# Sliding-window copy on one core: partitions by batch, channel half and 16-row band, and stores as 8 KB row scatters

## The chip, the core and the metric

The kernel runs on one core of a Trainium2 chip. The metric is device time in microseconds (µs), from the start of the program to its end. One execution was also taken by the hardware profiler; its span is the stretch that the profile covers.

## What is computed

The input is x of 16 batches, 64 channels, 64 rows and 64 columns in float32 (16.78 MB). A window of 8 by 8 moves over it with a stride of 4 in both directions, which gives 15 by 15 windows. The output holds each window for all channels (58.98 MB). No number is changed; the work is a gather.

```python
batch, c, h, w = (16, 64, 64, 64); window_size = 8; stride = 4
n_h = n_w = 15
for i in range(n_h):
    for j in range(n_w):
        result[:, i, j] = x[:, :, 4*i:4*i+8, 4*j:4*j+8]   # -> [16, 15, 15, 64, 8, 8]
```

In the output, one batch and one window (i, j) are 64 channels of 64 numbers that lie together: 16 KB. Neighbouring windows overlap, so each input number is written about 3.5 times.

## The kernel before

The 128 partitions stand for 16 batches times 8 groups of 8 channels. Tile `L` holds the whole input: each partition has 8 channels of 64 rows. Two loads on the SP queue fill it (L41 and L42): first the upper 32 rows of every channel, then the lower 32.

Two nested loops run over i and j. For each window VectorE copies the 8 channels by 8 rows by 8 columns of every partition from `L` into a packed tile `g` (L50). Then the tile is stored with one DMA of 256 KB (L51). In it each partition writes 2 KB that lie together in the output. The stores alternate between the SP and the ACT queue. 28 buffers of `g` go round, so the copy of window k waits until the store of window k-28 has landed. ScalarE computes nothing, GpSimd only sets a few constants at the start, and TensorE has no work.

A queue issues in order: a store on SP stands behind the two loads and behind every earlier store on SP.

Of the kernel before, what the change touches and what calls it, by code (L numbers as in the profile page):

```python
# [1 line left out]

# [4 lines left out]


@with_exitstack  # L10
def kernel(
    ctx: ExitStack,
    tc: tile.TileContext,
    x: bass.AP,
    window_size: int,
    stride: int,
    out: bass.AP,
):
    nc = tc.nc
    P = nc.NUM_PARTITIONS  # L20

    B, C, H, W = x.shape
    Bo, NH, NW, Co, WSo, WSo2 = out.shape
    WS = int(window_size)
    ST = int(stride)
    assert Bo == B and Co == C and WSo == WS and WSo2 == WS

    f32 = mybir.dt.float32

    CHI = P // B  # L30
    CLO = C // CHI
    assert CHI * B == P and CLO * CHI == C

    lpool = ctx.enter_context(tc.tile_pool(name="lpool", bufs=1))
    gpool = ctx.enter_context(tc.tile_pool(name="gpool", bufs=28))

    L = lpool.tile([P, CLO, H, W], f32)

    HHALF = H // 2
    x_v = x.rearrange("b (ch cl) h w -> b ch cl h w", ch=CHI)  # L40
    nc.sync.dma_start(out=L[:, :, 0:HHALF, :], in_=x_v[:, :, :, 0:HHALF, :])  # L41
    nc.sync.dma_start(out=L[:, :, HHALF:H, :], in_=x_v[:, :, :, HHALF:H, :])  # L42

    trig = [nc.sync, nc.scalar]
    k = 0
    for i in range(NH):
        for j in range(NW):
            g = gpool.tile([P, CLO, WS, WS], f32, name="g")
            src = L[:, :, i * ST : i * ST + WS, j * ST : j * ST + WS]
            nc.vector.tensor_copy(out=g[:, :, :, :], in_=src)  # L50
            trig[k % 2].dma_start(out=out[:, i, j, :, :, :], in_=g[:, :, :, :])  # L51
            k += 1


# [1 line left out]
_INS = ['x', 'window_size', 'stride']  # L56
_OUTS = [((16, 15, 15, 64, 8, 8), 'float32')]
#: Inputs that are plain numbers.
_NUMBERS = {'window_size': 8, 'stride': 4}


# [26 lines left out]
```

## Time and profile before

| | |
|---|---|
| Median of 9 runs | 220.88 µs (220.25 to 222.49) |
| The profiled execution: own time, span | 219.09 µs, 217.3 µs |
| Moved | 75.83 MB: 16.78 MB read, 58.98 MB written |
| Mean over the span | 349 GB/s |
| VectorE busy | 89.1 µs (41% of the span), 225 copies |
| ScalarE, TensorE busy | no instructions that count as busy |

In the views of the profile, "DMA share" is the mean busy share of the core's 16 DMA engines in a stretch, and may stand a little over 1 where packets overlap. "GB/s" is what they moved in it. A packet is one piece that lies together in memory at both ends: 8 KB in the loads and 2 KB in the stores here. A name with "q" (SPq, ACTq) is the queue on which an engine issues DMAs. The profiled execution lies 1.79 µs above its span, and 0.8% under the median of the runs.

### The profile page before, as it was taken

What the parts mean: (1) busy time and instruction counts of PE and PEld (TensorE: products, weight loads), DVE (VectorE), ACT (ScalarE), POOL (GpSimd) and SP (SyncE); (2) the same over time, 40 slices, a digit from 0 to 9 for tenths busy, and PEclk for the clock granted to TensorE, in tenths of its full rate; (3) what the DMA queues carried; (4) which work ended last, traced back from release to release, by engine and by line L of the source; (5) the groups of instructions that cost most, each with busy time, mean ns of one, the idle gap of its engine ahead of it and who ended that gap; (6) DMA issues with size and microseconds to landing.
All of it is one profiled execution on the core that took longest, in us unless ns stands there. A gap on an engine that the chain in (4) does not pass through costs nothing.

```text
span 217.3 us, 824 instructions
## 1 busy us (share of the span) xinstructions
DVE 89.1 (41%) x225; POOL 0.2 (0%) x4
## 2 busy tenths in 40 slices
DVE  0000791124532444554655545555564556550000
POOL 0000000000000000000000000000000000000000
DMA  6999999989995999999999999999999999999996
GB/s 210 425 427 419 425 417 426 421 314 322 330 332 172 294 304 351 359 363 358 357 369 354 361 347 358 351 350 350 347 358 342 352 356 359 351 362 352 330 348 235
DMA packets 34487, 75.83 MB, mean 349 GB/s; under 512 B 3632, under 2 KB 3632, under 8 KB 32432
## 3 DMA queue, kind: packets, MB, share of 16 engines
q1 hardware_dynamic: 18352, 46.41, 58.9%
q10 hardware_dynamic: 16128, 29.37, 39.6%
q14 instruction: 7, 0.06, 0.1%
HBM read 16.78 MB, written 58.98 MB: 349 GB/s over the span
## 4 chain that ended last, share of the span: by engine, by line
DMA 82%; DVE 7%; issue 1%; DVEq 0%; ACTq 0%
DMA out_dram<-g 72%; DMA L<-in_x_dram 10%; DVE g L50 7%; DVEq L50 0%; ACTq L51 0%
## 5 line engine op out<-in xcount | busy, mean ns | idle before, releaser
L50 DVE COPY g<-L 128x512 f32<-128x512 f32 x225 | 89.1, 425 | 107.0 <-DMA out_dram<-g 82.1
L69 POOL MEMSET const-bfloat16-1.0<- 128x1 bf16 x1 | 0.1, 102 | 0.0
L69 POOL MEMSET const-uint8-127<- 128x1 uint8 x1 | 0.1, 102 | 0.0
L69 POOL MEMSET const-float32-1.0<- 128x1 f32 x1 | 0.1, 99 | 0.0
L69 POOL MEMSET const-float32-0.0<- 128x1 f32 x1 | 0.1, 98 | 0.2 <-issue 0.2
## 6 DMA issues: line engine op xcount, KB each, us to landing
out_dram<-g SPq DMA_DIRECT2D x113, 256.0 KB, 5.5
out_dram<-g ACTq DMA_DIRECT2D x112, 256.0 KB, 5.1
L<-in_x_dram SPq DMA_DIRECT2D x2, 8192.0 KB, 33.8
```

The source lines that it names most:

```text
L50: nc.vector.tensor_copy(out=g[:, :, :, :], in_=src)
L69: nc = _bacc.Bacc("TRN2", target_bir_lowering=False, num_devices=1)
```

## The change

**Layout.** Partition p now stands for batch p/8, channel half (p/4) mod 2 and a band q = p mod 4 of 16 rows. Each partition of `L` holds 32 channels by 16 rows by 64 columns. 16 loads of 1 MB fill it: for each chunk of 8 channels (in the order 2, 0, 1, 3) one for each band, the even bands on SP and the odd ones on ACT. Such a load goes to every fourth partition, 32 of them, in pieces of 4 KB.

**Windows.** An instruction now makes four windows of one column j at once, one for each band: i = 4q + s with the slot s from 0 to 3. So there are 15 x 4 = 60 steps in place of 225. The slots 0 to 2 lie inside the band and are copied by ScalarE (L112). Slot 3 takes its upper 4 rows from the partition's own band (VectorE, L114) and its lower 4 from the next partition's first rows, through VectorE's `stream_shuffle` (L115). In slot 3 the band 3 has no window (i would be 15).

**Stores.** A step's tile is 8 KB in each partition, which lie together in the output. GpSimd stores it with an indirect DMA (L125): 128 rows of 8 KB, each to the row that `idx` names. `idx` is worked out once at the start by 11 small VectorE instructions on a 128x1 tile (L63 to L78). In slot 3 the rows of band 3 get a number beyond the bounds, and are not stored.

**Start and end.** The first 8 steps are made in two halves of 16 channels (stores of 0.5 MB with rows of 4 KB): the first halves need only the chunks 0 and 1. The second halves follow two by two between whole steps. The last two steps are stored from SP in 4 and 3 pieces of 32 partitions (L119). Their tiles reuse the buffers of the third and second last step before them. Nine buffers of 1 MB (`G_101` to `G_109`) go round.

The diff, without the arithmetic of `idx`:

```diff
-    nc.sync.dma_start(out=L[:, :, 0:HHALF, :], in_=x_v[:, :, :, 0:HHALF, :])
-    nc.sync.dma_start(out=L[:, :, HHALF:H, :], in_=x_v[:, :, :, HHALF:H, :])
-    trig = [nc.sync, nc.scalar]
-    for i in range(NH):
-        for j in range(NW):
-            g = gpool.tile([P, CLO, WS, WS], f32, name="g")
-            nc.vector.tensor_copy(out=g[:, :, :, :], in_=src)
-            trig[k % 2].dma_start(out=out[:, i, j, :, :, :], in_=g[:, :, :, :])
...
+    x_v = x.rearrange("b (ch cl) (hq r) w -> hq (b ch) cl (r w)", ch=CH, hq=HQ)
+    for k in (2, 0, 1, 3):
+        for q in range(HQ):
+            (nc.sync, nc.scalar)[q % 2].dma_start(
+                out=L[q::HQ, k * cw : (k + 1) * cw, :, :],
+                in_=x_v[q, :, k * cw : (k + 1) * cw, :],
+            )
...
+    order = [(j, s) for j in range(NW) for s in range(NSLOT)]
+    TAIL, BACK = 2, 3
...
+    def window(j, s, half):
...
+        if not last:
+            nc.scalar.copy(out=g, in_=L[:, cs, s * ST : s * ST + WS, cols])
+        else:
+            nc.vector.tensor_copy(out=g[:, :, 0:ST, :], in_=L[:, cs, s * ST : RB, cols])
+            nc.vector.stream_shuffle(out=g[:, :, ST:WS, :], in_=L[:, cs, 0:ST, cols], mask=nxt)
+        if (j, s) in order[-TAIL:]:
+            g_q = g.rearrange("(m q) c r w -> q m (c r w)", q=HQ)
+            for q in range(HQ - 1 if last else HQ):
+                free(nc.sync.dma_start(out=o_q[q * NSLOT + s, j], in_=g_q[q]))
+            return
...
+        st = nc.gpsimd.indirect_dma_start(
+            out=o,
+            out_offset=bass.IndirectOffsetOnAxis(ap=ix[:, 0:1], axis=0),
+            in_=g.rearrange("p c r w -> p (c r w)"),
...
+    EARLY = 8
+    for j, s in order[:EARLY]:
+        window(j, s, 0)
...
+    at -= 2 * BACK
+    for w in rest[-TAIL:]:
+        window(*w, None)
```

On the ACT queue the start reads as follows, before (-) and after (+). `L` is the input tile, `G_101` and so on are the nine store buffers, and the shapes are those of what is moved:

```order
-L51 DMA out_dram<-g 16x8x512 x112
...
+L52 DMA L<-in_x_dram 32x8x1024 x8
+L112 ACT_TABLE_LOAD
+L112 COPY G_101<-L 128x1024 x2
+L112 COPY G_102<-L 128x1024
+L112 COPY G_103<-L 128x1024 x2
+L112 COPY G_104<-L 128x1024
```

The 112 stores are gone from ACT. It now issues half of the loads, and then makes the copies of the slots 0 to 2.

On the GpSimd queue, which stored nothing before, the stores stand in this order behind the start (`idx_hlast` and `idx_h` are the row numbers of the half stores, with band 3 left out and with it; `idx` is that of the whole ones):

```order
8 L125 DMA out_dram<-G_102,idx_hlast 14400x1024 [waits DVE_49]
9 L125 DMA out_dram<-G_104,idx_hlast 14400x1024 [waits DVE_49]
10 L125 DMA out_dram<-G_101,idx_h 14400x1024 [waits Activation_49] x2
11 L125 DMA out_dram<-G_102,idx_h 14400x1024 [waits Activation_49]
12 L125 DMA out_dram<-G_103,idx_h 14400x1024 [waits Activation_49] x2
13 L125 DMA out_dram<-G_104,idx_h 14400x1024 [waits Activation_49]
14 L125 DMA out_dram<-G_105,idx_h 14400x1024 [waits DMASW0_49,Activation_49]
```

The two stores that VectorE makes come first, then six of ScalarE's; from the ninth store on, each also waits until the store eight places before it has landed.

On SP the stores of every other window are replaced by half of the loads and by the seven pieces at the end:

```order
-L41 DMA L<-in_x_dram 128x8x2048
-L42 DMA L<-in_x_dram 128x8x2048
-L51 DMA out_dram<-g 16x8x512 x113
...
+L52 DMA L<-in_x_dram 32x8x1024 x8
+L119 DMA out_dram<-G_102 16x2x2048 x4
+L119 DMA out_dram<-G_103 16x2x2048 x3
```

SP goes from 115 DMAs to 15, and its stores come last.

More of the change, by code (lines that the diff above doesn't have):

```diff
@@ L28 @@
     f32 = mybir.dt.float32
-    CHI = P // B
-    CLO = C // CHI
-    assert CHI * B == P and CLO * CHI == C
-    lpool = ctx.enter_context(tc.tile_pool(name="lpool", bufs=1))
[L35 to L41, printed above, removed]
-    nc.sync.dma_start(out=L[:, :, HHALF:H, :], in_=x_v[:, :, :, HHALF:H, :])
@@ L44 @@
-    trig = [nc.sync, nc.scalar]
-    k = 0
-    for i in range(NH):
-        for j in range(NW):
-            g = gpool.tile([P, CLO, WS, WS], f32, name="g")
[L49 to L52, printed above, removed]
+    i32 = mybir.dt.int32
+    ALU = mybir.AluOpType
+    HQ = 4
+    CH = P // (B * HQ)
+    CL = C // CH
@@ new lines @@
+    RB = H // HQ
+    NSLOT = RB // ST
+    NWIN = NH * NW
+    CFREE = CL * WS * WS
+    assert HQ == 4 and CH == 2 and WS == 2 * ST
+    lpool = ctx.enter_context(tc.tile_pool(name="lpool", bufs=1))
+    ipool = ctx.enter_context(tc.tile_pool(name="ipool", bufs=1))
+    gpool = ctx.enter_context(tc.tile_pool(name="gpool", bufs=1))
+    L = lpool.tile([P, CL, RB, W], f32)
+    x_v = x.rearrange("b (ch cl) (hq r) w -> hq (b ch) cl (r w)", ch=CH, hq=HQ)
+    NCH = 4
+    cw = CL // NCH
+    for k in (2, 0, 1, 3):
[4 more added lines that the diff above has]
+            )
@@ new lines, in itile @@
+    def itile(name):
+        return ipool.tile([P, 1], i32, name=name)
+    pi, tb, tq, tc_, idx, idx_last = (itile(n) for n in ("pi", "tb", "tq", "tc", "idx", "idx_last"))
+    nc.gpsimd.iota(pi[:, :], pattern=[[0, 1]], base=0, channel_multiplier=1)
+    nc.vector.tensor_scalar(out=tb[:, :], in0=pi[:, :], scalar1=3, scalar2=None, op0=ALU.logical_shift_right)
+    nc.vector.tensor_scalar(out=tc_[:, :], in0=pi[:, :], scalar1=2, scalar2=1, op0=ALU.logical_shift_right, op1=ALU.bitwise_and)
+    nc.vector.tensor_scalar(out=tq[:, :], in0=pi[:, :], scalar1=HQ - 1, scalar2=None, op0=ALU.bitwise_and)
@@ new lines @@
+    nc.vector.tensor_scalar(out=tb[:, :], in0=tb[:, :], scalar1=float(NWIN * CH), scalar2=None, op0=ALU.mult)
+    nc.vector.tensor_tensor(out=tb[:, :], in0=tb[:, :], in1=tc_[:, :], op=ALU.add)
+    nc.vector.tensor_scalar(out=tc_[:, :], in0=tq[:, :], scalar1=float(NSLOT * NW * CH), scalar2=None, op0=ALU.mult)
+    nc.vector.tensor_tensor(out=idx[:, :], in0=tb[:, :], in1=tc_[:, :], op=ALU.add)
+    nc.vector.tensor_scalar(out=tq[:, :], in0=tq[:, :], scalar1=float(HQ - 1), scalar2=float(2 * B * NWIN * CH), op0=ALU.is_equal, op1=ALU.mult)
@@ new lines @@
+    nc.vector.tensor_tensor(out=idx_last[:, :], in0=idx[:, :], in1=tq[:, :], op=ALU.add)
+    HCL = CL // 2
+    idx_h, idx_hlast = itile("idx_h"), itile("idx_hlast")
+    for d, e in ((idx_h, idx), (idx_hlast, idx_last)):
+        nc.vector.tensor_scalar(out=d[:, :], in0=e[:, :], scalar1=2.0, scalar2=None, op0=ALU.mult)
+    o_v = out.rearrange("b i j (ch cl) r w -> (b i j ch) (cl r w)", ch=CH)
+    o_h = out.rearrange("b i j (ch cl) r w -> (b i j ch) (cl r w)", ch=2 * CH)
+    nxt = [min(p + 1, 31) for p in range(32)]
@@ new lines, with free @@
+    order = [(j, s) for j in range(NW) for s in range(NSLOT)]
+    TAIL, BACK = 2, 3
+    o_q = out.rearrange("b i j (ch cl) r w -> i j b ch (cl r w)", ch=CH)
+    def free(st):
+        tc.declare_no_dep(st.ins, group="stores", reason="each store writes rows of its own")
+        tc.add_to_no_dep_group("stores", st.ins)
+    UNITS = 18
+    G = [gpool.tile([P, 2 * HCL, WS, WS], f32, name=f"G{n}") for n in range(UNITS // 2)]
+    at = 0
+    def window(j, s, half):
+        nonlocal at
+        cols = slice(j * ST, j * ST + WS)
+        last = s == NSLOT - 1
+        if half is None:
+            n, c0 = 2, 0
+            at += at % 2
+        else:
+            n, c0 = 1, half * HCL
+        u = at % UNITS
+        at += n
+        cs = slice(c0, c0 + n * HCL)
+        g = G[u // 2][:, u % 2 * HCL : (u % 2 + n) * HCL, :, :]
+        if not last:
+            nc.scalar.copy(out=g, in_=L[:, cs, s * ST : s * ST + WS, cols])
+        else:
+            nc.vector.tensor_copy(out=g[:, :, 0:ST, :], in_=L[:, cs, s * ST : RB, cols])
[5 more added lines that the diff above has]
+            return
+        if half is None:
+            o, ix = o_v, (idx_last if last else idx)
+        else:
+            o, ix = o_h, (idx_hlast if last else idx_h)
+        st = nc.gpsimd.indirect_dma_start(
+            out=o,
+            out_offset=bass.IndirectOffsetOnAxis(ap=ix[:, 0:1], axis=0),
+            in_=g.rearrange("p c r w -> p (c r w)"),
+            in_offset=None,
+            element_offset=(s * NW + j) * CH * CFREE + (half or 0) * HCL * WS * WS,
+            bounds_check=B * NWIN * CH * (1 if half is None else 2) - 1,
+            oob_is_err=False,
+        )
+        free(st)
@@ L56 @@
+    EARLY = 8
+    for j, s in order[:EARLY]:
+        window(j, s, 0)
+    late = list(order[:EARLY])
+    rest = list(order[EARLY:])
+    while late:
+        for w in late[:2]:
+            window(*w, 1)
+        for w in rest[:2]:
+            window(*w, None)
+        late, rest = late[2:], rest[2:]
+    for w in rest[:-TAIL]:
+        window(*w, None)
+    at -= 2 * BACK
+    for w in rest[-TAIL:]:
+        window(*w, None)
 _INS = ['x', 'window_size', 'stride']
```

## The prediction

> **What bounds the kernel now.** I read the page first, then the chain of waits, then the busy time by stretches, and last the issues of the stores.
>
> ```profile
> DVE 89.1 (41%) x225; POOL 0.2 (0%) x4
> DMA packets 34487, 75.83 MB, mean 349 GB/s; under 512 B 3632, under 2 KB 3632, under 8 KB 32432
> HBM read 16.78 MB, written 58.98 MB: 349 GB/s over the span
> DMA out_dram<-g 72%; DMA L<-in_x_dram 10%; DVE g L50 7%; DVEq L50 0%; ACTq L51 0%
> L50 DVE COPY g<-L 128x512 f32<-128x512 f32 x225 | 89.1, 425 | 107.0 <-DMA out_dram<-g 82.1
> ```
>
> VectorE works 41% of the span and waits 82.1 µs for stores to free its buffers; 82% of the chain that ended last is DMA. So the rate of the transfers bounds it, and the question is what that rate is in each stage. The stretches say it (columns: from:to, length, VectorE busy and count, GpSimd busy and count, a clock that does not matter here, DMA share, GB/s):
>
> ```profile
> 2.00:3.00 1.00, 0.00 (x0) 0.00 (x0) 1.00 0.95 156
> 3.00:4.00 1.00, 0.00 (x0) 0.00 (x0) 1.00 0.87 360
> 10.00:23.00 13.00, 0.00 (x0) 0.00 (x0) 1.00 1.01 423
> 23.00:45.00 22.00, 11.10 (x32) 0.00 (x0) 1.00 1.02 423
> 45.00:50.00 5.00, 1.71 (x4) 0.00 (x0) 1.00 0.82 285
> 50.00:100.00 50.00, 22.48 (x58) 0.00 (x0) 1.00 0.96 315
> 100.00:200.00 100.00, 53.81 (x131) 0.00 (x0) 1.00 1.03 355
> 200.00:215.00 15.00, 0.00 (x0) 0.00 (x0) 1.00 1.00 340
> 215.00:216.00 1.00, 0.00 (x0) 0.00 (x0) 1.00 0.46 174
> 216.00:217.30 1.30, 0.00 (x0) 0.00 (x0) 1.00 0.00 0
> ```
>
> Four things are to be seen. Loading runs at 423 GB/s. Storing alone runs at 355, with the engines just as full: a store packet simply takes longer for its bytes. In 45 to 100 the engines are not full. And little moves in the first 4 µs and the last 2.
>
> Packet times follow as share x 16 engines x bytes / rate. A load packet takes 1.01 x 16 x 8192 / 423 = 313 ns; a store packet takes 1.03 x 16 x 2048 / 355 = 95 ns, where a quarter of 313 would be 78. A line through both gives 22 ns for a packet and 35.5 ns for each KB (28 GB/s for one engine).
>
> The start: 156 + 360 KB by 4.0 µs are 1.2 µs at 423, so 2.8 µs are lost. The end: 174 KB after 215 are 0.5 µs at 355, so 1.8 µs are lost. The hole: 285 for 5 µs and 315 for 50, against 355, lose 1.0 + 5.6 = 6.6 µs. Its cause is an order on a queue:
>
> ```profile
> SPq L51 <- DMA out_dram<-g: 77.8, 28, 56.2
> L51 SPq DMA_DIRECT2D out_dram<-g x113: 538/1213/1757, 58.4 to 212.6; - x113
> L51 ACTq DMA_DIRECT2D out_dram<-g x112: 546/728/1427, 24.1 to 195.4; - x112
> 0.73 0.68 SPq L41 DMA_DIRECT2D L<-in_x_dram  x1
> ```
>
> SP issues its first store only at 58.4 µs, so ACT stores alone until then. An issue (min/median/max in ns) takes 0.54 to 1.76 µs. From the first load's issue at 0.73 to its first bytes (156 of 423 GB/s in the slice 2:3, so from 2.6) pass 1.9 µs.
>
> **The change part by part.**
>
> *Loads, 16.78 MB.* Each is now 4 KB packets to 32 partitions, where it was 8 KB to all 128. By the line a 4 KB packet takes 22 + 142 = 164 ns, which is 400 GB/s. Bounds: 355, the rate of the stores, which also split 16 ways by batch with partitions stepped, and 423. I take 390, between the line and the low end: 43.0 µs (39.7 to 47.3). Sixteen issues of 0.68 µs on two queues are 5.4 µs a queue and run ahead of the bytes.
>
> [...]
>
> *Stores, 58.98 MB.* 225 stores of 2 KB packets become 50 whole and 16 half scatters, and 7 pieces from SP. Almost all bytes go as 8 KB packets from 128 partitions. By the line such a packet takes 313 ns, or 423 GB/s; if the slowness of stores lies in writing and not in the packet, it stays at 355. Nothing before shows an 8 KB store. I take 415: the loads are its nearest row in packet size and partitions, less 2% for the half scatters with 4 KB rows. That is 142 µs (139.4 to 166.1).
>
> *The seam.* The first halves need the chunks 2, 0 and 1, three quarters of the loads: 2.8 + 12.58/0.390 = 35.1 µs. VectorE's copy and shuffle of 128x512 take 0.43 µs each by L50's 425 ns (the shuffle is not in the trace: 0.43 to 0.9), the issue 1.2, the way to the first bytes 1.9: stores begin near 39 µs. By then 14.1 MB are loaded, and 2.7 MB of chunk 3 with 3.9 MB of half stores keep the engines going for 16 µs, to 55. Chunk 3 has landed by about 50 even if it shares the engines equally; a copy, an issue and the way add 0.85 + 1.2 + 1.9 = 4 µs. So one stream hands over to the other with about a microsecond to spare: 0 to 4 µs of hole, I take 1.5, in place of the 6.6 now. `ACT_TABLE_LOAD` and the eleven index instructions stand there while the loads run, and cost nothing while VectorE's two stores go first.
>
> *ScalarE's copies.* A 128x2048 copy has four times the elements of L50's: 1.7 µs at that speed; ScalarE has no row, so up to twice that, 3.4. Three stand in four steps, 5.1 µs (10.2), against 3.75 MB / 415 = 9.0 µs of storing. They are covered by the stores in flight, and only at the upper end would they lead. VectorE's share, 0.85 to 1.7 µs for each half of a slot-3 step, is under 3.4 in 9.0 µs. The 107.0 µs that VectorE idles now are proof that copying has room. [...]
>
> *GpSimd's issues.* 66 stand in order on one queue. No row has their price; SP's and ACT's bound it at 0.54 and 1.76, I take 1.2. A whole store needs 2.5 µs of the engines, so they are hidden behind eight stores in flight. In the half phase 0.5 MB need 1.25 µs, so above 1.3 they lead there for a while: up to 0.5 µs x 16 = 8 µs at 1.76, most of it beside the loads.
>
> *The end.* The tile of step (14,2) waits until (13,3) has landed; 2 MB, 5 µs of work, are in flight then. Copy 1.7 + issue 0.7 + way 1.9 = 4.3 µs fit into that; the last tile follows 2.5 µs later in the same way. I take 1 µs of hole (0 to 3) beside the 1.8 at the end.
>
> *Sum.* Start 2.8 + loads 43.0 + stores 142 + seam 1.5 + last steps 1 + end 1.8 = 192.1 µs of span; plus 1.8 around it (219.09 - 217.3) makes 193.9, against the profiled execution's 219.09. The median of the runs lies 0.8% above that execution, so 194 to 195.5 in such terms. I say 194. With everything at 423 and no hole it is 179.3 + 2.8 + 1.8 + 1.8 = 186.
>
> **The rivals.**
>
> *Stores stay at 355 GB/s*, because writing is what is slow. For it: in the pure store stage the rate hardly moves from 355 over 100 µs. Against it: beside loads, the engines move 423. Time: 2.8 + 43.0 + 166.1 + 1.5 + 1 + 1.8 + 1.8 = 218; with loads as fast as now, 214.7; without seam and end holes, 212. The line as drawn would be wrong, and only the 6.6 µs hole would be gained.
>
> [...]
>
> *GpSimd's issues lead* (the slower case). Nothing bounds their price surely: GpSimd stores nothing before. From the first issue at 36 µs, 66 issues of p, then about 4 µs for the last steps, 5 for the last bytes and 3.6 at the end and around: 48.6 + 66p. It is slower than before from p = 2.6 µs; at 3.0 it is 247. Against it: the dearest issue seen is 1.76. All of them behind each other is the point: on two queues before, on one now.
>
> [...]
>
> *Loads collapse.* If the stepped partitions halve the loading rate to 212 GB/s, loads take 79 µs, and the time is 230. No row shows that; the stores before, with a similar step, held 355.
>
> *No gain shows*: the store rate rises a little and the holes and slower loads eat it: 219 to 222.
>
> **How the numbers follow.** The forecast (186 to 204) gets 0.62: packet size and partition split both speak for it. Stores at or near 355 (204 to 218, most of it 210 to 218) get 0.24. No gain gets 0.03. GpSimd leading past 2.6 µs gets 0.07, collapsed loads 0.04. The likeliest gives 194. The range 185 to 213 holds the forecast's 0.62 and some two thirds of the second case. A measurement of this kernel tells about 0.5% from no change (219.8 to 222): faster 0.86, same 0.03, slower 0.11.
>
> **What would show it.** In the changed kernel's stretches: about 390 GB/s up to 35 µs; over 400 from 60 µs to the end at a share near 1; no stretch of the seam under 300. ScalarE near 45 x 1.7 = 80 µs busy, waiting for stores to land. If the stores stay near 355 with a full share, the second case holds. If the share falls under 0.9 in mid-span and copies sit waiting while GpSimd's queue waits for nothing, it is the issue. A first stretch under 300 with a full share would be the loads.

## The result and the profile after

The changed kernel takes 193.53 µs (median of 10 runs, 193.21 to 194.05) against 220.88 before (31 runs): a ratio of 0.877, 95% interval 0.874 to 0.879. The forecast was 194. The profiled execution took 193.48 µs, 1.78 above its span of 191.7.

The page of the changed kernel, first the busy time and the queues, then the groups:

```profile
DVE 30.2 (16%) x62; ACT 86.2 (45%) x52; POOL 64.4 (34%) x71
DMA packets 14196, 75.80 MB, mean 395 GB/s; under 512 B 1936, under 2 KB 1936, under 8 KB 7952
q0 software_dynamic: 9504, 57.15, 73.1%
HBM read 16.78 MB, written 62.65 MB: 414 GB/s over the span
L112 ACT COPY G<-L 128x2048 f32<-128x2048 f32 (+1 forms) x51 | 85.0, 1695 | 59.3 <-DMA out_dram<-G,idx_last 25.0
L125 POOL DMA_INDIRECT out_dram<-G,idx x38 | 36.8, 970 | 49.6 <-DMA out_dram<-G,idx 45.6
```

No engine is busy for half of the span, and ScalarE and GpSimd wait for stores to land, as VectorE did before. The transfers bound this kernel too, at 395 GB/s over the span in place of 349. The stretches of the changed kernel (from:to, length, busy time of VectorE, ScalarE and GpSimd with counts, clock, DMA share, GB/s):

```profile
0.00:4.00 4.00, 1.23 (x11) 0.00 (x0) 0.32 (x5) 1.00 0.41 128
4.00:36.00 32.00, 0.00 (x0) 0.00 (x0) 0.00 (x0) 1.00 1.03 411
36.00:68.00 32.00, 7.95 (x18) 27.82 (x22) 22.59 (x23) 1.00 1.02 419
68.00:168.00 100.00, 19.13 (x30) 56.52 (x30) 41.52 (x43) 1.00 1.01 411
168.00:180.00 12.00, 0.00 (x0) 0.06 (x1) 0.00 (x0) 1.00 1.00 411
180.00:184.00 4.00, 1.65 (x3) 1.83 (x1) 0.00 (x0) 1.00 0.62 244
184.00:188.00 4.00, 0.25 (x1) 0.00 (x0) 0.00 (x0) 1.00 0.84 256
188.00:191.70 3.70, 0.00 (x0) 0.00 (x0) 0.00 (x0) 1.00 0.56 188
```

Three things are to be seen. Storing runs at 411 GB/s, as the loads do, and no longer at 355. The hole between 45 and 100 µs has gone: where loads and stores meet, 36 to 68, the rate is the highest of all. And the end is worse: from 180 µs on 2.70 MB move (4 x 244 + 4 x 256 + 3.7 x 188), 6.6 µs of work at 411, in 11.7 µs.

### The profile page after: what moved, and what is told of

Read it like the earlier page. It is cut to its first block, busy times and chain, and to the rows that moved or that the text cites. A ratio compares the mean times of both kernels' runs of the same rounds, so it can differ in the third digit from the quotient of the medians.

```text
span 191.7 us, 458 instructions
## 1 busy us (share of the span) xinstructions
DVE 30.2 (16%) x62; ACT 86.2 (45%) x52; POOL 64.4 (34%) x71
## 3 DMA queue, kind: packets, MB, share of 16 engines
q0 software_dynamic: 9504, 57.15, 73.1%
HBM read 16.78 MB, written 62.65 MB: 414 GB/s over the span
## 4 chain that ended last, share of the span: by engine, by line
DMA 66%; issue 25%; POOL 3%; DVE 1%; POOLq 0%; DVEq 0%; PEldq 0%
DMA out_dram<-G,idx 57%; DMA out_dram<-G,idx_h 9%; POOL out_dram L125 3%; DVE G L115 1%; DVE G L114 0%; POOLq L125 0%; POOL pi L62 0%; DVEq L114 0%; PEldq L182 0%
## 5 line engine op out<-in xcount | busy, mean ns | idle before, releaser
L112 ACT COPY G<-L 128x2048 f32<-128x2048 f32 (+1 forms) x51 | 85.0, 1695 | 59.3 <-DMA out_dram<-G,idx_last 25.0
L125 POOL DMA_INDIRECT out_dram<-G,idx x38 | 36.8, 970 | 49.6 <-DMA out_dram<-G,idx 45.6
L114 DVE COPY G<-L 128x1024 f32<-128x1024 f32 (+1 forms) x17 | 10.9, 639 | 152.9 <-DMA out_dram<-G,idx 88.5
L115 DVE STREAM_SHUFFLE G<-L 128x1024 f32<-128x1024 f32 (+1 forms) x17 | 19.5, 1148 | 0.0
L125 POOL DMA_INDIRECT out_dram<-G,idx_hlast x4 | 4.0, 1001 | 37.6 <-DVE G L115 36.7
L125 POOL DMA_INDIRECT out_dram<-G,idx_last x12 | 11.6, 964 | 11.7 <-DVE G L115 6.9
L125 POOL DMA_INDIRECT out_dram<-G,idx_h x12 | 11.7, 975 | 3.7 <-issue 2.7
L63 DVE TENSOR_SCALAR tb<-pi 128x1 int32<-128x1 int32 x1 | 0.2, 154 | 1.0 <-POOL pi L62 1.0
L115 DVE LOAD_MASK_SELECT G<-L x17 | 0.2, 13 | 0.0
L78 DVE TENSOR_SCALAR idx_hlast<-idx_last 128x1 int32<-128x1 int32 x1 | 0.2, 154 | 0.0
L78 DVE TENSOR_SCALAR idx_h<-idx 128x1 int32<-128x1 int32 x1 | 0.2, 154 | 0.0
```

The lines of the kernel that those rows point to most:

```text
L63: nc.vector.tensor_scalar(out=tb[:, :], in0=pi[:, :], scalar1=3, scalar2=None, op0=ALU.logical_shift_right)
L78: nc.vector.tensor_scalar(out=d[:, :], in0=e[:, :], scalar1=2.0, scalar2=None, op0=ALU.mult)
L112: nc.scalar.copy(out=g, in_=L[:, cs, s * ST : s * ST + WS, cols])
L114: nc.vector.tensor_copy(out=g[:, :, 0:ST, :], in_=L[:, cs, s * ST : RB, cols])
L115: nc.vector.stream_shuffle(out=g[:, :, ST:WS, :], in_=L[:, cs, 0:ST, cols], mask=nxt)
L125: st = nc.gpsimd.indirect_dma_start(out=o, out_offset=bass.IndirectOffsetOnAxis(ap=ix[:, 0:1], axis=0), in_=g.rearrange("p c r w -> p (c r ...
```

## The experiments

The prediction left two causes for the old 355 GB/s: small packets, and the way in which a store is split (16x8x512 here). All rates below are from the same 60 µs of store stage, 100 to 160.

**The split alone.** Two kernels change nothing in the kernel before but where its stores go (the second also leaves out the last window). In the first, row p of each store goes to p x 450 KB, so that all 128 rows have one stride; the DMA is then made as 128x512 in place of 16x8x512.

```diff
+    o_f = out.rearrange("b i j c r w -> (b i j c r w)").rearrange("(p n) -> p n", p=P)
-            trig[k % 2].dma_start(out=out[:, i, j, :, :, :], in_=g[:, :, :, :])
+            trig[k % 2].dma_start(out=o_f[:, k * WN : (k + 1) * WN], in_=g.rearrange("p c r w -> p (c r w)"))
```

> The kernel before, but each store writes its 2 KB rows to other places: row p of window k goes to p x 450 KB + k x 2 KB, 128 rows at one stride, so the DMA is made as 128x512 and no longer as 16x8x512. The output therefore holds the right bytes in wrong places. Same queues, packets, sizes, loads and copies. Theory A (the split of 16x8x512 over the engines is what was slow): the store stage rises from 355 towards 400 GB/s and the time falls by 10 to 20 us, to 200 to 211. Theory B (SP and ACT stores of 2 KB are slow whatever the split): 355 GB/s, 219 to 222 us.

The second puts the rows at nearly the same places, but with an odd stride after each eighth, which brings 16x8x512 back.

```diff
+    RS = NH * NW * WN - 64
+    o_f = out.rearrange("b i j c r w -> (b i j c r w)").rearrange("(a n) -> a n", a=16)
+    o_f = o_f[:, 0 : 8 * RS].rearrange("a (c n) -> a c n", c=8)
```

> As the run with 128 rows at one stride, but after each eighth row the stride is 2 KB longer, and a row 256 bytes shorter, so that the rows don't merge and the DMA is made as 16x8x512 again; the last window is not stored (0.4% of the bytes). The places in memory are nearly those of the 128x512 run. Theory A (the split): 355 GB/s again, about 220 us. Theory C (where the rows lie in memory is what made the difference): as fast as the 128x512 run.

Measured: 203.94 µs with 128 rows (ratio 0.920, 0.916 to 0.925), and 220.48 with 16x8 (0.998, 0.994 to 1.001). The store stage of the first and of the second (VectorE's and GpSimd's busy time stand ahead of the clock):

```profile
100.00:160.00 60.00, 32.63 (x84) 0.00 (x0) 1.00 1.04 381
```

```profile
100.00:160.00 60.00, 33.83 (x82) 0.00 (x0) 1.00 1.03 354
```

Same queues, packets, sizes and nearly the same addresses: 381 against 354. So the split costs 7% of the store rate, and neither 2 KB packets nor the SP and ACT queues explain the old 355 whole. The second run also rules out theory C. With 128 rows an issue on SP became shorter too (median 416 ns against 1213); the packet times below show that the gain lies in the transfers themselves.

**Packet size with the old split.** The changed kernel's layout, with every tile stored as four pieces of 32 partitions from SP and ACT. The batches stay in the outer dimension (16x2x2048), and the packets are 8 KB.

```diff
-    TAIL, BACK = 2, 3
+    TAIL, BACK = 60, 0
+                eng = nc.scalar if q % 2 and not last else nc.sync
+                free(eng.dma_start(out=o_q[q * NSLOT + s, j], in_=g_q[q]))
-    EARLY = 8
+    EARLY = 0
```

> All stores go as pieces of 32 partitions from SP and ACT (256 KB each, 16 engines by batch, as before the change), but with 8 KB packets; no half steps at the start. Theory A (packet size sets the store rate): the store stage runs at about 410 GB/s; with the first store only after all loads (43.7 us, and 3 us of hole) the time is about 196 us. [...]

Measured: 228.15 µs (ratio 1.032, 1.026 to 1.037), slower than the kernel before. Its store stage:

```profile
100.00:160.00 60.00, 9.53 (x15) 31.58 (x17) 0.00 (x0) 1.00 0.98 342
```

The twin with a gap after each 2 KB of the tile (16x8x512 again, by the same pieces):

```diff
+    SPL = 4
+    G = [gpool.tile([P, SPL, CL // SPL * WS * WS + 16], f32, name=f"G{n}") for n in range(UNITS // 2)]
+            g_q = gp.rearrange("(m q) k x -> q m k x", q=HQ)
```

> As the run with 8 KB pieces, but the tiles have a gap after each 2 KB, so that the same bytes go from the same partitions by the same 256 KB pieces in 2 KB packets. The copies are made in four parts for each tile, which adds some 0.7 us of ScalarE for each step. Theory A (packet size): about 355 GB/s in the store stage, about 218 us. Theory B (split): the same as with 8 KB packets.

Its two runs lie apart, at 221.98 and 228.43 µs, so no ratio and no rate are taken from it; it does not show that 8 KB pieces (228.15) gain anything. With 342 against 355 GB/s, 8 KB packets are no faster than 2 KB under the batch split: theory A, on which the forecast's store term stood, falls for this split.

**Packet size with the 128-row split.** The changed kernel's layout and copies, stored from SP and ACT as 128 rows of 8 KB at one stride. No scatter and no half steps.

```diff
+    o_f = out.rearrange("b i j c r w -> (b i j c r w)").rearrange("(p n) -> p n", p=P)
+        n = j * NSLOT + s
+        eng = (nc.scalar, nc.sync)[s % 2]
+        free(eng.dma_start(out=o_f[:, n * CFREE : (n + 1) * CFREE], in_=g.rearrange("p c r w -> p (c r w)")))
```

> The changed kernel's layout, loads and copies, but no scatter and no half steps: SP and ACT store each tile as 128 rows of 8 KB at one stride, 1 MB a DMA (right bytes, wrong places; 56 of 60 steps with all 128 rows, 99.6% of the bytes). Theory A (the rate comes from 128 rows over the engines and 8 KB packets, not from GpSimd): 405 to 425 GB/s in the store stage, about 193 us. Theory B (SP and ACT can't store 8 KB packets faster, as the 340 GB/s of the pieces could also mean): 340 to 381 GB/s, 205 us or more.

Measured: 190.87 µs (0.863, 0.857 to 0.869), with the first store only after all loads and 56 of the 60 steps stored. Its store stage, and then that of the changed kernel:

```profile
100.00:160.00 60.00, 11.53 (x18) 33.11 (x18) 0.00 (x0) 1.00 1.01 419
```

```profile
100.00:160.00 60.00, 12.73 (x21) 34.15 (x18) 23.80 (x25) 1.00 1.01 410
```

So the four cells are:

| store stage, GB/s | 2 KB packets | 8 KB packets |
|---|---|---|
| 16 batches outermost | 355 (before), 354 | 342 |
| 128 rows | 381 | 419 from SP and ACT, 410 by scatter |

Only the pair 381 and 354 differs in the split alone. The run with 342 also stores 32 partitions at a time, and the runs with 419 and 410 store 1 MB at a time in place of 256 KB, which no run separates from the packet size. GpSimd is not what makes the stores fast (419 without it): in the real output batch, channel half and band lie at uneven strides, and the scatter is a way to hand over 128 separate rows all the same.

The traces also hold the time of every single packet, which the views above do not print. For the stores from 100 to 160 µs, and the loads from 10 to 36 ("long" is over 1.5 times the usual 84, 159 or 309 ns for 2, 4 or 8 KB):

| packets | mean, ns | long |
|---|---|---|
| 2 KB stores, 16 batches outermost (before; second kernel) | 94; 94 | 10.7%; 10.2% |
| 2 KB stores, 128 rows | 88 | 0.1% |
| 8 KB stores, 16 batches outermost | 370 | 14.9% |
| 8 KB stores, 128 rows (SP and ACT; changed kernel's scatters) | 315; 322 | 0.1%; 0.1% |
| 8 KB loads, 128 partitions (before) | 313 | none |
| 4 KB loads, every fourth partition (changed kernel) | 164 | none |

So the batch split does not slow every store packet. It makes one in ten of 2 KB, and one in seven of 8 KB, much longer: a twentieth of the 2 KB packets before took 168 ns or more, twice the usual. The mean of 94 against 88 is the 7% of the rate. The usual times alone give 9 ns for a packet and 37.5 ns for each KB: undisturbed, four packets of 2 KB take 336 ns and one of 8 KB 309.

**The hole.** The kernel before, with its loads issued by GpSimd.

```diff
-    nc.sync.dma_start(out=L[:, :, 0:HHALF, :], in_=x_v[:, :, :, 0:HHALF, :])
-    nc.sync.dma_start(out=L[:, :, HHALF:H, :], in_=x_v[:, :, :, HHALF:H, :])
+    nc.gpsimd.dma_start(out=L[:, :, 0:HHALF, :], in_=x_v[:, :, :, 0:HHALF, :])
+    nc.gpsimd.dma_start(out=L[:, :, HHALF:H, :], in_=x_v[:, :, :, HHALF:H, :])
```

> The kernel before with its two loads issued by GpSimd, so that SP's first store no longer stands behind them. Theory A (the order on SP makes the hole between 45 and 100 us): stores of both queues start at about 24 us, the hole of 6.6 us goes, and the time is about 214 us. Theory B (the hole comes from two stores streams that fall out of step for another reason): no change, 220 to 222 us.

Measured: 212.45 µs (0.961, 0.956 to 0.965). What SP's stores waited for longest was 56.2 µs before; in this run SP's first store waits only for VectorE's first tile (columns: total, times, longest):

```profile
SPq L51 <- DVE g L50: 108.3, 103, 24.7
SPq L51 <- DMA out_dram<-g: 30.9, 32, 5.8
```

Theory A holds: 8.4 µs (220.88 less 212.45) for two words in the code. Then this edit and that to 128 rows at one stride at once:

> The kernel before with both edits: loads issued by GpSimd, and stores as 128 rows of 2 KB at one stride (right bytes, wrong places). Theory A (hole and split are two separate losses): about 19.6 MB by 50 us as in the run with GpSimd's loads, then 56.3 MB at 381 GB/s, and 3.6 us at the end and around: 201 us. What remains to the changed kernel's 193.5 is then the packet size, 381 against about 411 GB/s. Theory B (the two overlap): 203 to 204 us, no better than the 128x512 run.

Measured: 199.58 µs (0.903, 0.898 to 0.908). That is 1.4 µs under theory A's number, but the two savings do not simply add. Alone the loads' edit saves 8.4 µs and the split 16.9 (220.88 less 203.94), 25.3 in sum; together they save 21.3. The hole and the split overlap by 4 µs. The hole was in part the split: with 128 rows and the loads still on SP, these stretches (the first line is the kernel before, the others are the 128-row kernel) move more.

```profile
50.00:60.00 10.00, 5.03 (x12) 0.00 (x0) 1.00 0.99 322
```

```profile
45.00:50.00 5.00, 2.14 (x5) 0.00 (x0) 1.00 0.87 331
50.00:60.00 10.00, 5.46 (x13) 0.00 (x0) 1.00 1.02 379
50.00:100.00 50.00, 26.55 (x69) 0.00 (x0) 1.00 0.98 362
```

Against its own 381 that kernel loses 3.1 µs in the hole (0.25 + 0.95 MB), where the prediction counted 6.6 before. The changed kernel's 193.5 is 6 µs below this run. From 381 to 410 its stores gain 58.98/381 - 58.98/410 = 10.9 µs, of which slower loads and the poorer end give back some.

**GpSimd's issues.** Every whole scatter as two halves, 116 in place of 66.

```diff
     for w in rest[:-TAIL]:
-        window(*w, None)
+        window(*w, 0)
+        window(*w, 1)
```

> The changed kernel with every whole scatter made as two half scatters with rows of 4 KB: 116 issues on GpSimd in place of 66, at 1.27 us from one to the next, 147 us. Theory A (neither packet size nor the issues bound the scatters): 193 to 195 us. Theory B (the line of the prediction, 164 ns for a 4 KB packet, 400 GB/s): 197 us. Theory C (issues lead): over 200 us.

Measured: 198.00 µs (0.893, 0.889 to 0.898): near the number of theory B, but GpSimd's issues lead. The store stage, what GpSimd's queue waited for, and the way from issue to landing in this kernel:

```profile
100.00:160.00 60.00, 13.07 (x36) 37.21 (x36) 45.57 (x47) 1.00 1.00 388
```

```profile
POOL out_dram L125 <- issue: 21.3, 70, 0.3
```

```profile
DMA to landing us min/median/max: 4.6/5.4/7.3
```

The same way in the kernel without pieces at the end (below), where all but the first 16 scatters are whole:

```profile
DMA to landing us min/median/max: 6.9/18.3/19.4
```

A step carries 58.98/60 = 0.983 MB on the mean, a half 0.4915; at one issue each 1.27 µs (0.97 of work and 0.30 between) that is 387 GB/s, and 388 were moved. The way from issue to landing has shrunk from 18.3 to 5.4 µs, and 70 issues waited for nothing but the issue before. GpSimd leads here, theory C's mechanism, at a smaller price than its "over 200". A busy share of 1.00 did not show it. The lead is narrow: the 4 KB packets took 168 ns on the mean, which at that share is 390 GB/s, so the engines had hardly any room left. The loads moved 411 in 4 KB packets; whether stores of 4 KB could stays open.

**The end.** Four kernels change only the last steps. First, the last two tiles take the two oldest buffers, and no longer wait for late stores:

```diff
-    TAIL, BACK = 2, 3
+    TAIL, BACK = 2, 0
```

> The last two steps take the two oldest buffers, so their tiles no longer wait for the third and second last store. In the changed kernel the last 11.7 us move 2.70 MB, 6.6 us of work at 411 GB/s, so 5.1 us are lost there. Theory A (the wait for the buffer makes the hole): the hole goes, only about 2 us are lost at the end, and the time falls from 193.5 to about 190.5. Theory B (the small pieces from SP and their way to the first bytes make it): the time stays within 1 us of 193.5.

Measured: 198.11 µs (0.896, 0.893 to 0.899). Both theories fall: the change made it slower. The stretch in which SP's pieces run beside the scatters:

```profile
170.00:180.00 10.00, 0.98 (x1) 0.00 (x0) 0.00 (x0) 1.00 1.00 341
180.00:190.00 10.00, 0.00 (x0) 0.00 (x0) 0.00 (x0) 1.00 0.86 313
```

Pieces with the batch split pull the whole stage down to 341 GB/s while they last. From 172 to 188 µs 34% of their packets are long, and 10% of those of the scatters beside them, where one of 399 was from 160 to 168. Then no pieces at all:

```diff
-        if (j, s) in order[-TAIL:]:
+        if False:
```

> The changed kernel with all 60 steps stored by scatters, none in pieces from SP. Theory A (pieces with the batch split are slow and slow down whatever runs beside them, as the run with the two oldest buffers showed: 311 to 361 GB/s for 16 us): the stage holds about 411 GB/s to the end, the 5.1 us lost there fall to 2 or 3, and the time is about 191 us. Theory B (a scatter's last bytes land late, and that is what the pieces hide): 193 to 196 us.

Measured: 194.55 µs (0.878, 0.875 to 0.882), in theory B's range:

```profile
176.00:184.00 8.00, 0.00 (x0) 0.00 (x0) 0.00 (x0) 1.00 1.00 416
184.00:188.00 4.00, 0.00 (x0) 0.00 (x0) 0.00 (x0) 1.00 0.52 219
188.00:189.00 1.00, 0.00 (x0) 0.00 (x0) 0.00 (x0) 1.00 0.12 49
189.00:192.60 3.60, 0.00 (x0) 0.00 (x0) 0.00 (x0) 1.00 0.00 0
```

The rate holds to 184 µs. Then the share is 0.52 for 4 µs: the packets' times show eight or nine under way at a time from 184.4 to 188. That reads as half of the engines done and the other half at work, though no row names an engine. The last packet ends at 188.7, and 3.9 µs pass until the span ends. In the changed kernel, where SP's pieces end the work, it is 1.3 (190.4 to 191.7). Last, two ways to issue the pieces earlier, from SP and ACT in turn:

```diff
-                free(nc.sync.dma_start(out=o_q[q * NSLOT + s, j], in_=g_q[q]))
+                eng = nc.scalar if q % 2 else nc.sync
+                free(eng.dma_start(out=o_q[q * NSLOT + s, j], in_=g_q[q]))
```

> The changed kernel with the seven last pieces issued from SP and ACT in turn. Theory A (0.86 us for each issue on SP alone starves the engines between 182 and 186 us, where they moved 201 to 266 GB/s): the pieces come twice as fast, and about 1 us is gained, 192.5 us. Theory B (the last tile's wait for its buffer and VectorE's 2 us set the end): within 0.4 us of 193.5.

and on top of it the last tiles waiting for one store less:

```diff
-    TAIL, BACK = 2, 3
+    TAIL, BACK = 2, 4
```

> As the run before it, and the last two tiles wait one store less: for the fourth and third last scatter. Theory A (the earlier start fills the stretch from 179.5 us, where half of the engines have run dry): about 1.5 us less than with the third last, 191 to 192 us. Theory B (more pieces beside scatters slow these, as with the two oldest buffers): 194 us or more.

Measured: 193.33 (0.875, 0.871 to 0.879) and 193.06 (0.873, 0.870 to 0.877). The first is theory B; the second lies between its two theories. Both intervals overlap the changed kernel's. 193.06 is 0.2% under it, less than can be told apart, so no version is shown to beat it.

## Why the prediction was right, point by point

*The time* was right, to 0.5 µs, and so were the sign and the bound: transfers lead, every copy is covered. That it came so close is in part luck: the terms below were off by up to 2.3 µs each, and cancelled.

*Loads*: 411 GB/s against 390 taken, within 355 to 423: 40.8 µs in place of 43.0. The line's 164 ns for a 4 KB packet came out; its 400 GB/s took a share of 1.00, where 1.03 was seen. The low end of 355 was that of stores whose batches each lie on eight neighbouring partitions, not on stepped ones. The 3% under the 423 of before is the packet size: the usual 159 and 309 ns give 412 and 424 GB/s at a share of 1. The stepped partitions cost nothing that shows. Loads did not collapse.

*The seam*: no hole, where 1.5 µs were taken. The first scatter starts at 37.67 µs, and the loads that are left fill the engines until the half stores take over.

*Stores*: 411 against 415 taken, 143.5 µs in place of 142. The rate was right and its reason half wrong. The step that failed is the line through the packet times, which put the difference of 95 and 78 ns down to the packet. With 128 rows a 2 KB packet took 88 ns: some 6 of the 17 ns were the split, and a packet's own cost, by the usual times, is 9 ns and not 22. With that line the 8 KB pieces should have run at 423; they ran at 342, with 370 ns a packet in place of 313. What the forecast leaned on beside it, that the old loads went to all 128 partitions and the new scatter does too, is what the runs bear out. The rival "stores stay at 355, because writing is slow" falls: 419 were written from SP and ACT.

Why the split makes some packets long was not shown: which engine served which partition is in no row. Loads show no such loss: those to every fourth partition have no long packets (164 ns on the mean), though the 8 KB pieces, stored from the same 32 partitions each, have 14.9%. The forecast's 0.62 counted the partition split in as well; no row of before shows what it costs, and the runs put it at 354 against 381 GB/s.

*ScalarE*: 85.0 µs of copies, where 80 were forecast; a whole one takes 1897 ns, between the ends of 1.7 and 3.4.

```profile
L112 ACT COPY G<-L 128x2048 f32<-128x2048 f32 x39 | 73.8, 1897 | 57.0 <-DMA out_dram<-G,idx_last 25.0 <-DMA out_dram<-G,idx 17.2 <-DVE G L115 13.3
```

*GpSimd's issues*: 1.27 µs each against 1.2. They are hidden, and the run with halves shows from where they lead: 1.27 µs against what one store needs of the engines (1.2 µs for half a step). The slower rival needed 2.6 µs an issue, twice what was measured.

*The end* was mis-sized: 5.1 µs lost (11.7 less 6.6) in place of 2.8. The forecast saw the wait for the buffers, but not that the share falls to half early (0.52 from 180 to 182 µs), nor that pieces run at the old rate (342 GB/s where all stores are pieces). Loads and seam came out 4 µs better than taken (2.2 and 1.5), stores and end 4 worse (1.5 and 2.3).

## What to carry to other kernels

Read the store rate of a stage beside the shape in which the DMA was made. Where the outermost dimension is not the 128 partitions (16x8 here), try to give the DMA 128 rows, before packet size: the same bytes at nearly the same addresses went from 354 to 381 GB/s, and only with 128 rows did 8 KB packets in 1 MB DMAs reach 410 to 419. Loads showed no such loss here (no long packets, at 164 ns for 4 KB). Do not add up savings that were measured one by one: two here gave 21.3 µs of 25.3. And price each queue's issues against the bytes that one issue carries: 1.27 µs were free for 1 MB and led for 0.5 MB, with the engines at a share of 1.01 and 1.00.

## What the runs showed of the hardware that was not expected

At the end of a long row of scatters the share falls to 0.52 for about 4 µs, with eight or nine packets under way at a time (above). In the changed kernel about sixteen are under way from 168 to 178 µs and eight or nine from 180 to 183. So half of the engines seem to finish early; why is open.

Rows left out by the bounds still make packets, but hardly any bytes: q0 has 9504 packets, 66 stores of 128 rows and 16 more each, while its 57.15 MB are 50 whole and 16 half scatters (60.82 MB) less 3.67 MB, the 32 left-out rows in each of 14 slot-3 steps. Of its packets 1568 carry 4 bytes: 16 for each store, and the 512 left-out rows (32 in each of 16 slot-3 scatters). The page's "written 62.65 MB" counts the left-out rows.

An issue on GpSimd took only a little longer with a VectorE copy beside it:

```profile
60.85 1.04 POOL L125 DMA_INDIRECT out_dram<-G,idx  x1 [0.30 <-issue]
61.08 0.69 DVE L114 COPY G<-L 128x1024 f32<-128x1024 f32 x1 [3.82 <-DMA out_dram<-G,idx]
```

The copy lies wholly within the issue. It took its usual 0.69 µs, and the issue 0.08 µs more than the usual 0.96. Over all 50 whole scatters an issue took 960 ns at the least and 1044 at the most.
